# Paged attention of the sample rows starts at the output projection instead of beside the prompt's attention

## The chip, the cores and the metric

The kernel runs on one core of a Trainium2 chip. The metric is the device time of one execution in microseconds (us). Before the change three executions took 1454.08, 1442.74 and 1447.46 us; the median is 1447.46 us. A further execution was profiled.

## What is computed

One layer of a hybrid decoder, in float32, for two groups of rows at once.

- The **prompt**: 16 meta tokens and 1024 rows. RMSNorm, one input projection, differential attention with 4 heads of two softmax maps each (causal, with ALiBi), a gated depthwise convolution of width 31 with LayerNorm and swish, an output projection over both, a norm and the residual, then a SwiGLU feed-forward part (1024 to 2816 to 1024).
- The **samples**: 8 sequences with one new row each, which go through the same layer, but whose attention reads a paged cache: 32 pages of 128 keys per sequence. A page of keys and a page of values are 128 x 512 floats (256 KB) each, found through a page table. Cut to its core:

```
k_past = ck[page_table]; v_past = cv[page_table]
s = q . k * HEAD_DIM**-0.5 - slope * (q_pos - k_pos)
p = softmax(s);  a = p[map 0] - lam * p[map 1];  o = a @ v
```

All pages together are 512 transfers of 256 KB, 134 MB, of the 264 MB that the kernel moves.

## The kernel before

The prompt's work has four stages, written out in program order. First the projection stripes for the convolution and the convolution itself. Then the attention loop at the end of `tile_layer`: 32 blocks `n`, eight blocks of 128 query rows for each of four heads; between the blocks, `chunk_to` puts the remaining projection stripes of q, k and v, and these are all out by n = 22. Then the output projection, eight calls of `c_one` (the first at n = 31, inside the loop, the others behind it). Last the feed-forward part, `ffn`, which calls a helper `fill` 133 times between its groups of matmuls. Large products are made of three matmuls on the rounded value H and the rest L of each operand (`mm3`, L149 to L151).

In one attention block (`attn`) TensorE makes the scores (L507, L508), VectorE adds the bias and finds the extreme (L509), ScalarE takes the exponential (L515), VectorE joins the two maps (L526), TensorE transposes (L534), ScalarE copies (L538) and TensorE multiplies with the values (L548). GpSimd has the small powers of the norms (L125, L564), the L parts of some weights (L140) and of the keys (L300).

The samples' paged attention is a generator, `dec_units`, that other code advances by steps. A step is one pair of pages:

- **Keys** (128 steps): SyncE issues two page loads (`page_pair`, L665), GpSimd multiplies 128x1024 elements by the query (L679), VectorE sums them by head (L689).
- **Softmax**, once a sequence has its 16 key pairs: `dec_max` (L697 to L706, with a reduction over the partitions on GpSimd, L706), `dec_exp` (L711, L712), `dec_total` (L716).
- **Values** (128 steps): two page loads and, for two pairs side by side, eight matmul records with 8 columns of weights (L731).

The first 23 steps are keys only; from then on two value pairs alternate with two key pairs. When the generator is through, `fill` advances the sample rows' own layer (`sample_units`, 81 steps that read 512 KB of weights each).

`dec_step(rate)` adds `rate` to an account and takes as many whole steps. It is called in three places: in the attention loop from block `db` on, with `rate_b` of the head; in every `c_one`, with `rate_c`; in every `fill`, with `rate_d`. `fill` goes on with `rate_s` for the sample layer. The steps are put into the program at raised priority (400 instructions), and a planner that simulates a timeline orders the instructions of each engine. Each engine then works through its own list in that order and waits where an operand is late. The first load of each pair stands in the order behind the matmul last marked. Page buffers come from `kv`: four buffers until `kv_n[1]` is set behind the attention loop, then six more, which are the buffers `p` of the prompt's probabilities.

Of the kernel before, what the change touches and what calls it, by code (L numbers as in the profile page):

```python
# [46 lines left out]
def tile_layer(ctx: ExitStack, tc: tile.TileContext, I, O, cfg):  # L47
# [1339 lines left out]
    lag=7, rlag=1, elag=2,  # L1387
    xn_g=(), wi_first=1, wi_e=(13, 17), sq=0,
    behind=-400, w0=7, w1=7, wi_n=1, anchor=1, wi_v=(8, 9, 10, 11, 12), taps=11, conv=400, r2_g=1, hb=5,
    vgrp=2, fing=5, ml_g=0, fend=22, cst=0, db=3, cn=6, scn=12, wo0=27, wor=2, c0=7,  # L1390
    at=8, slabs=35, kv=4, p=6, dve_mul=0, rate_b=(1, 1.25, 1, 0.75), rate_c=1, rate_d=2.45, rate_s=2.2,
    ffn_l=lambda nc: nc.vector,
)
_INS = [
# [39 lines left out]
```

## Time and profile before

| | |
|---|---|
| median of three executions | 1447.46 us (1442.74 to 1454.08) |
| the profiled execution | 1442.33 us |
| its span, first to last instruction | 1440.6 us |
| TensorE (PE) busy | 1353.5 us, 94% |
| VectorE (DVE) busy | 876.8 us, 61% |
| ScalarE (ACT) busy | 552.2 us, 38% |
| GpSimd (POOL) busy | 560.5 us, 39% |
| moved by DMA | 264.35 MB, mean 183 GB/s |

The span is the profiled execution less 1.7 us around it. PE is busy nearly all the time, so the places to look at are those where it isn't. An engine's wait is named by what it waited for; a wait of an engine other than PE costs time only where PE in the end waits for it. Each engine works in order, so what stands behind a waiting instruction waits too.

### The profile page before, as it was taken

How to read it: one execution, taken by the hardware profiler on the slowest of the kernel's cores; microseconds unless marked ns; L12 is line 12 of the kernel's file. 1: busy time of each engine (PE TensorE's matmuls, PEld its weight loads, DVE VectorE, ACT ScalarE, POOL GpSimd, SP SyncE). 2: the span in 40 equal slices, each digit the busy share in tenths (PEclk: the TensorE clock that was granted, in tenths of full speed). 3: DMA queues.
4: the chain of work that ended last, by engine and by line, in shares of the span. 5: the costliest groups of instructions: out<-in, count | busy, mean ns of one | idle time of the engine just before them, and what ended most of it. 6: DMA issues, size and time to landing. Idle time of an engine off the chain costs nothing.

```text
span 1440.6 us, 21580 instructions
## 1 busy us (share of the span) xinstructions
PE 1353.5 (94%) x6960; PEld 1054.5 (73%) x6960; DVE 876.8 (61%) x1403; ACT 552.2 (38%) x1112; POOL 560.5 (39%) x351
## 2 busy tenths in 40 slices
PE   5999899979858999999999989999999999999997
PEld 5999799978746787777777667677676765666666
DVE  5689996945765467465748366565754265462158
ACT  7566978697855345212222121222122112211122
POOL 4598866444444123545445455454530000000023
PEclk9999999999979999999999999999999999999999
DMA  8221024226515538678777868687687656664454
GB/s 253 78 59 39 28 64 145 81 88 199 160 61 183 176 125 283 221 241 278 260 244 235 260 202 262 229 273 248 206 267 231 224 159 217 220 202 125 146 190 176
DMA packets 199678, 264.35 MB, mean 183 GB/s; under 512 B 16423, under 2 KB 99816, under 8 KB 199557
## 3 DMA queue, kind: packets, MB, share of 16 engines
q1 hardware_dynamic: 188912, 254.40, 54.1%
q10 hardware_dynamic: 10653, 8.57, 1.9%
q8 instruction: 55, 0.90, 0.3%
q14 instruction: 58, 0.48, 0.1%
HBM read 245.92 MB, written 17.48 MB: 183 GB/s over the span
## 4 chain that ended last, share of the span: by engine, by line
PE 61%; DMA 2%; issue 2%; DVE 2%; SPq 2%; POOL 1%; ACT 0%; POOLq 0%; DVEq 0%; ACTq 0%
PE pg L149 5%; PE pu L149 5%; PE pg L150 5%; PE pu L150 5%; PE pu L151 5%; PE pg L151 5%; PE dn L149 5%; PE dn L150 5%; PE dn L151 5%; PE pv L731 4%; PE mo L151 2%; PE mo L149 2%; PE mo L150 2%; DMA k<-in_cache_k 1%; POOL k L679 1%
## 5 line engine op out<-in xcount | busy, mean ns | idle before, releaser
L679 POOL TENSOR_TENSOR k<-k,qB 128x1024 f32<-128x1024 f32 x128 | 317.8, 2499 | 257.1 <-DMA k<-in_cache_k 212.0
L689 DVE TENSOR_REDUCE s<-k 128x16 f32<-128x1024 f32 x128 | 155.0, 1213 | 106.9 <-POOL k L679 106.8
L955 ACT CAST wH<-wr 128x1024 fp32r<-128x1024 f32 x66 | 69.1, 1049 | 249.1 <-DVE wL L957 142.6
L149 PE MATMUL dn<-wH,aH 128*128 128x512 f32 x352 | 141.2, 405 | 4.4 <-DVE y L998 2.7
L150 PE MATMUL dn<-wL,aH 128*128 128x512 f32 x352 | 140.9, 400 | 0.0
L149 PE MATMUL pu<-hH,wH 128*128 128x512 f32 x352 | 140.3, 399 | 0.5 <-DVE y L998 0.5
L151 PE MATMUL dn<-wH,aL 128*128 128x512 f32 x352 | 140.7, 400 | 0.0
L149 PE MATMUL pg<-hH,wH 128*128 128x512 f32 x352 | 140.4, 399 | 0.0
L151 PE MATMUL pu<-hH,wL 128*128 128x512 f32 x352 | 138.6, 395 | 1.5 <-DVE sm2n_t L123 1.5
L150 PE MATMUL pu<-hL,wH 128*128 128x512 f32 x352 | 139.5, 397 | 0.0
L150 PE MATMUL pg<-hL,wH 128*128 128x512 f32 x352 | 139.3, 396 | 0.0
L151 PE MATMUL pg<-hH,wL 128*128 128x512 f32 x352 | 139.2, 395 | 0.0
L957 DVE TENSOR_TENSOR wL<-wr,wH 128x1024 fp32r<-128x1024 f32 x66 | 97.1, 1471 | 38.0 <-ACT wH L955 21.6
L998 DVE TENSOR_TENSOR y<-dn,y 128x512 f32<-128x512 f32 x144 | 95.0, 684 | 35.4 <-PE dn L151 34.9
L414 POOL TENSOR_TENSOR cb<-cb 128x512 f32<-128x512 f32 x80 | 102.9, 1318 | 17.7 <-ACT cb L413 9.9
L423 DVE SCALAR_TENSOR_TENSOR acc<-u,cw,acc 128x512 f32<-128x512 f32 x144 | 98.8, 749 | 0.2
L1070 POOL TENSOR_TENSOR y<-y,wfpost 128x512 f32<-128x512 f32 x10 | 17.4, 1754 | 205.2 <-ACT ft L1068 205.1
L149 PEld LDWEIGHTS dn<-wH,aH 128*128 128x128 f32 x352 | 67.3, 192 | 31.2 <-DVE y L998 6.2
L981 ACT CAST aH<-sg 128x512 fp32r<-128x512 f32 x44 | 27.3, 621 | 163.2 <-DVE sg L974 163.1
L149 PEld LDWEIGHTS pu<-hH,wH 128*128 128x128 f32 x352 | 66.1, 188 | 27.8 <-issue 12.0
L149 PEld LDWEIGHTS pg<-hH,wH 128*128 128x128 f32 x352 | 66.1, 188 | 27.4 <-issue 11.6
L150 PEld LDWEIGHTS dn<-wL,aH 128*128 128x128 f32 x352 | 66.9, 190 | 25.1 <-issue 10.3
(581 smaller groups left out, 2947.3 us busy)
## 6 DMA issues: line engine op xcount, KB each, us to landing
k<-in_cache_k SPq DMA_DIRECT2D x256, 256.0 KB
v<-in_cache_v SPq DMA_DIRECT2D x256, 256.0 KB
wr<-in_w_gate SPq DMA_DIRECT2D x22, 512.0 KB
wr<-in_w_up SPq DMA_DIRECT2D x22, 512.0 KB
wr<-in_w_down SPq DMA_DIRECT2D x22, 512.0 KB
sd<-in_w_down SPq DMA_DIRECT2D x22, 512.0 KB
sw_gate<-in_w_gate SPq DMA_DIRECT2D x20, 512.0 KB
sw_up<-in_w_up SPq DMA_DIRECT2D x20, 512.0 KB
```

The lines of the kernel that those rows point to most:

```text
L149: T.matmul(out, lhsT=wH, rhs=xH, start=first, stop=False)
L150: T.matmul(out, lhsT=wH, rhs=xL, start=False, stop=False)
L151: mark(T.matmul(out, lhsT=wL, rhs=xH, start=False, stop=last))
L414: G.tensor_tensor(accp, accp, t, op=ALU.add)
L423: V.scalar_tensor_tensor(dst, src, cw[:, ct, k : k + 1], acc, op0=ALU.mult, op1=ALU.add)
L679: x = G.tensor_tensor(kt, kt, qB.unsqueeze(1).to_broadcast([P, 2, 512]), op=ALU.mult)
L689: x = V.tensor_reduce(s.rearrange("p a c -> p (a c)"), kt.rearrange("p a (c d) -> p (a c) d", d=HD), axis=AX.X, op=ALU.add)
L731: x = T.matmul(pv[32 * g : 32 * g + 8, :], lhsT=a[:, q + i, :], rhs=vt[:, i, :], start=q + i < 4, stop=q + i >= NPG - 4, tile_position=(0, ...
L955: S.copy(H[:, :1024], raw[:, :1024])
L957: V.tensor_tensor(L[:, :1024], raw[:, :1024], H[:, :1024].bitcast(F32), op=ALU.subtract)
L981: S.copy(aH, sg)
L998: V.tensor_tensor(y[b][:, ws], o, y[b][:, ws], op=ALU.add)
```

## The change

Four numbers change. With `db=32` the condition `n >= cfg["db"]` holds for no block of the loop, whose last n is 31, so `dec_step` is not called there any more and `rate_b` is without use. The call in `c_one` takes two steps instead of one, the one in `fill` 2.65 instead of 2.45, and the sample layer goes at 2.3 steps per `fill` instead of 2.2. No operation is added or removed.

```diff
-    vgrp=2, fing=5, ml_g=0, fend=22, cst=0, db=3, cn=6, scn=12, wo0=27, wor=2, c0=7,
-    at=8, slabs=35, kv=4, p=6, dve_mul=0, rate_b=(1, 1.25, 1, 0.75), rate_c=1, rate_d=2.45, rate_s=2.2,
+    vgrp=2, fing=5, ml_g=0, fend=22, cst=0, db=32, cn=6, scn=12, wo0=27, wor=2, c0=7,
+    at=8, slabs=35, kv=4, p=6, dve_mul=0, rate_b=(1, 1.25, 1, 0.75), rate_c=2, rate_d=2.65, rate_s=2.3,
```

The calls that these numbers steer, which stay as they are:

```python
        if n >= cfg["db"]:
            dec_step(cfg["rate_b"][h])
...
        dec_step(cfg["rate_c"])        # the end of c_one
...
        if dst["done"]:
            credit[0] += cfg["rate_s"]
...
        else:
            dec_step(cfg["rate_d"])    # in fill
```

## Rows read from the trace of the kernel before

**Rows 1.** Windows: length, busy us (count) of PE, PEld, DVE, ACT, POOL, clock, DMA, GB/s.
```profile
195.00:380.00 185.00, 171.27 (x1163) 164.96 (x1163) 122.89 (x296) 151.14 (x381) 90.14 (x60) 0.98 0.37 118
380.00:451.00 71.00, 42.61 (x250) 37.16 (x251) 49.31 (x120) 42.91 (x115) 32.95 (x17) 0.78 0.46 147
451.00:580.00 129.00, 129.00 (x616) 102.34 (x616) 75.35 (x128) 53.17 (x129) 29.86 (x25) 1.00 0.59 196
580.00:1140.00 560.00, 551.43 (x2546) 392.18 (x2545) 319.04 (x346) 112.34 (x150) 241.11 (x102) 0.99 0.74 244
1140.00:1430.00 290.00, 284.51 (x1320) 190.47 (x1320) 148.90 (x222) 57.54 (x97) 24.14 (x20) 0.99 0.54 179
```

**Rows 2.** PE in order of time, 380 to 460 us: start, length, operation [idle before].
```profile
402.07 1.16 PE L548 MATMUL o<-V,ats 128*128 128x128 f32 x8 [3.25 <-ACT ats L538]
...
415.57 0.75 PE L507 MATMUL S<-R,L 128*128 128x456 f32 x1 [5.23 <-DVE nm L509]
...
421.49 0.66 PE L507 MATMUL S<-R,L 128*128 128x352 f32 x1 [4.79 <-DVE nm L509]
...
444.52 0.47 PE L571 MATMUL oT<-ident,oh 128*128 128x128 f32 x1 [5.46 <-ACT oh L566]
```

**Rows 3.** DVE in order of time, the same stretch.
```profile
400.65 0.43 DVE L711 TENSOR_TENSOR s<-s,dg 128x264 f32<-128x264 f32 x1 [4.37 <-POOL dg L706]
...
413.27 1.22 DVE L689 TENSOR_REDUCE s<-k 128x16 f32<-128x1024 f32 x1 [5.75 <-POOL k L679]
...
415.94 4.78 DVE L526 SCALAR_TENSOR_TENSOR p<-p,cc,p 128x400 f32<-128x400 f32 x2
...
425.21 1.17 DVE L526 SCALAR_TENSOR_TENSOR p<-p,cc,p 128x400 f32<-128x400 f32 x2
...
437.73 5.43 DVE L526 SCALAR_TENSOR_TENSOR p<-p,cc,p 128x400 f32<-128x400 f32 x2
```

**Rows 4.** POOL in order of time, the same stretch.
```profile
410.91 4.64 POOL L679 TENSOR_TENSOR k<-k,qB 128x1024 f32<-128x1024 f32 x2
415.51 2.35 POOL L140 TENSOR_TENSOR wo3L<-wo3r,wo3H 128x1024 fp32r<-128x1024 f32 x1
...
437.48 2.36 POOL L679 TENSOR_TENSOR k<-k,qB 128x1024 f32<-128x1024 f32 x1
```

**Rows 5.** Groups by line (busy, mean ns | idle): 195 to 460 us twice, 460 to 580 us.
```profile
L679 POOL TENSOR_TENSOR k<-k,qB 128x1024 f32<-128x1024 f32 x26 | 61.7, 2383 | 19.3 <-DMA k<-in_cache_k 19.0
...
L689 DVE TENSOR_REDUCE s<-k 128x16 f32<-128x1024 f32 x24 | 29.1, 1214 | 8.8 <-POOL k L679 8.8
...
L679 POOL TENSOR_TENSOR k<-k,qB 128x1024 f32<-128x1024 f32 x8 | 20.2, 2535 | 22.9 <-DMA k<-in_cache_k 22.9
```

**Rows 6.** Waits of SP's queue, 380 to 460 us: total us, times, longest.
```profile
SPq L665 <- DVE s L689: 18.8, 2, 9.8
SPq L665 <- PE pv L731: 18.5, 1, 18.5
```

**Rows 7.** Groups by line, POOL, 580 to 1140 us.
```profile
L679 POOL TENSOR_TENSOR k<-k,qB 128x1024 f32<-128x1024 f32 x95 | 238.3, 2527 | 216.0 <-DMA k<-in_cache_k 171.3 <-issue 21.3 <-DVE s L689 12.8
```

**Rows 8.** Groups by line, DVE: 700 to 1050 us, then 1150 to 1390 us.
```profile
L957 DVE TENSOR_TENSOR wL<-wr,wH 128x1024 fp32r<-128x1024 f32 x27 | 46.3, 1716 | 11.1 <-PE pg L150 5.3 <-PE pu L150 3.9 <-ACT wH L955 1.2
...
L957 DVE TENSOR_TENSOR wL<-wr,wH 128x1024 fp32r<-128x1024 f32 x19 | 23.1, 1217 | 17.4 <-ACT wH L955 16.9 <-PE pu L151 0.5
```

**Rows 9.** Waits of DVE, 460 to 1141 us: total us, times, longest.
```profile
DVE s L689 <- POOL k L679: 98.0, 38, 6.7
```

**Rows 10.** The chain that ended last, in order of time: start, length, what.
```profile
831.80 4.39 DMA k<-in_cache_k
...
838.64 1.22 DVE s L689
...
862.82 0.97 PE pv L731 x8
...
1403.42 0.96 PE sd L1233 x4
```

## The prediction, made before the change was run

> **What bounds the kernel now.** I began with the busy shares and the 40 slices of the page, then asked for windows by stage. Five stages follow from them [rows 1]. PE is idle 13.7 us of 185 in the mixed part of the attention loop, and 28.4 us of 71 (71.00 less 42.61) in its last part, from 380 to 451 us, where no projection stripe is left to fill it and its clock was granted at 0.78 of full. In the output projection it is not idle at all. In the feed-forward part it is idle 8.6 us of 560 while pages are read, and 5.5 us of 290 afterwards. So the time is PE's work plus these holes, and a change that moves work without changing it can only win or lose in the holes. The reader should see that half of all idle time of PE from 195 us on lies in the 71 us before the output projection.
>
> The timelines of PE, DVE and POOL say what makes the holes there [rows 2 to 4]. Page work stands in the orders of DVE and POOL between the prompt's steps, and the prompt waits for it. The groups by line give its amount [rows 5], the waits of SP's queue and of DVE, with POOL's groups, its state in the other stages [rows 6, 7, 9].
>
> **How many steps move.** Before, the loop takes 5 + 10 + 8 + 6 = 29 steps (blocks 3 to 7 at 1, then eight blocks each at 1.25, 1 and 0.75) and the eight `c_one` take 8: 37, and 219 are left for the feed-forward part. After, the condition is true for no block, the eight `c_one` take 16, and 240 are left. At 2.45 and 2.65 per `fill` that is 89.4 and 90.6 fills of 133. The sample layer's 81 steps then take 36.8 and 35.2 fills, so it ends at fill 126.2 before and 125.8 after. The end of the program is thus left alone: the last sample matmul, now at 1403 us [rows 10], keeps its distance from it. I cost that at nothing; the cover is the six or seven fills behind it.
>
> **The attention loop, what is taken out.** 26 products of 2.38 us on POOL and 24 sums of 1.21 us on DVE, 62 and 29 us [rows 5], the first softmax, and one group of value matmuls, 0.97 us like each of these [rows 10]. Most of this ran beside other work. On the path are these holes of PE:
>
> - **First softmax.** DVE waits 4.37 us for the reduction on POOL [rows 3], ScalarE's copies stand behind that, and PE is idle 3.25 us [rows 2]. Gain 3.2.
> - **A sum in front of the bias.** DVE stands 5.75 us at a sum whose product is late on POOL [rows 3], the next L509 is behind it, and PE is idle 5.23 us [rows 2]. Gain 5.2.
> - **A stretched L526.** A pair of them takes 1.17 us at 425 us and 4.78 us at 416 us [rows 3], while POOL computes wo3L, which had stood behind two page products of 4.64 us [rows 4]. Without these, wo3L is over before DVE gets there. PE's hole is 4.79 us [rows 2]; bounds 0 and 4.8, I take 4.0, since 4.64 us of POOL's lateness are removed.
> - **The last L526 and the last norm.** 5.43 us beside a page product of 2.36 us and the last weight split [rows 3, 4]; PE's hole is 5.46 us [rows 2]. Bounds 0 and 5.5; the split stays, so I take the product, 2.4.
> - **The mixed part.** Bounds 0 and its 13.7 us of holes [rows 1]. PE is 93% busy there, so I take 2.0.
> - **Clock.** 42.6 us of PE work ran at 0.78 in the last part [rows 1]. All of it at full would give 42.6 x 0.22 = 9.4 us; nothing is the other end. Holes remain, and latency counts more than rate here, so I take 2.0.
>
> That is 18.8 us. **What is late next** is ScalarE, busy 42.9 of these 71 us [rows 1], and it has no page work worth naming. It must follow DVE more closely than now, so I give back 2: **16.8 us gained**.
>
> The stretch of L526 has a rule behind it. In the Trainium skill, "SBUF — State Buffer", section "SBUF: two separate sides", a VectorE operation with two SBUF inputs and a GpSimd operation exclude each other for a whole instruction. The trace agrees: 4.78 against 1.17 us [rows 3]. By the rule alone each of the 26 products could hold DVE for its full 2.38 us, 62 us in the loop; as DVE has slack there, the sum by the rows stands at 16.8. The same rule speaks against the change further on (third rival).
>
> **SP's queue.** The 58 or so page loads of the loop go. In the last part SP stood 37 us on page loads that waited for a free buffer [rows 6], with loads of the output weights and of the first block's inputs behind them. These come earlier. Bounds 0 and some us; the holes counted above contain what of it reached PE, so I add nothing.
>
> **The output projection.** 16 steps instead of 8, all keys: 16 products where 8 ran [rows 5], so 19 us more on POOL (busy 30 of 129) and 10 us more on DVE (75 of 129) [rows 1]. 16 more page loads stand on SP's queue among the next block's inputs; the longest wait of such a load for a sum was 9.8 us [rows 6], and an input is asked for one block, about 13 us, ahead. Bounds 0 and 9.8; I take 0, since PE has no hole there now and the cover is that one block. Without it a late input would stop PE at once. Four groups of value matmuls leave this stage, 3.9 us of PE, and return later: nothing.
>
> **The feed-forward part.** The value group that ran in a hole costs its 0.97 us now: +1.0. The pace per fill is 2.65 / 2.45 = 1.08 of before. DMA is busy 0.74 of the page part at 244 GB/s [rows 1]. Pages are 219 x 0.524 MB / 560 us = 205 of these, so after it is some 261 GB/s and 0.79. PE's holes of 8.6 us grow at least in proportion: +0.7. The upper bound is in the second rival. The waits show how near the edge this is: POOL stands 171 us for key pages [rows 7], and DVE 98 us at sums for POOL [rows 9], which reach PE seldom, as around 832 us, where a page, its sum and PE follow each other [rows 10].
>
> **Sum.** 16.8 - 1.0 - 0.7 = 15.1, some 1 us of SP's earlier loads not counted. The profiled execution took 1442.3 us, 5.1 under the median. 1447.5 - 15.1 gives 1432.4, and I round the uncounted part in: **1431 us**.
>
> **The rivals.**
>
> 1. **The freed time was not on the path.** The last part is held by the chain from scores over exponential to transposes, and ScalarE's 43 us with PE's round trips fill the 71 us anyway. For it: ScalarE stands in the chain of each block. Against it: three of PE's holes end at once with page work [rows 2, 3]. Gain 16.8 falls to some 3: 1447.5 - 3 + 1.7 = 1446.
> 2. **Late pages in the feed-forward part (slower).** A page buffer comes free only when its sum or its matmul is done, so 10 buffers bound the pace. If 219 steps in 560 us is already the most that this loop can do, 240 steps need 614 us, and the 90.6 fills would by themselves take 567: up to 47 us lost, so 1431 + 47 - 1 = 1477. It decides from a loss of 16 us on, that is, when the loop does less than 240 / 583 = 0.41 steps per us against 0.39 now. For it: POOL is behind the pages most of the time [rows 7]. Against it: DMA is not full, and between 451 and 580 us, with 0.59 of DMA busy, nothing holds PE. Half of the loss would give 1454.
> 3. **Half the gain is taken back.** 17 products more run beside the feed-forward part (112 against 95). A split of a weight takes 1.72 us beside the products and 1.22 us without [rows 8], so DVE loses up to 0.5 us for each, 8.5 us, and the sums take 21 us more. DVE is busy 319 of 560 us and waits 98 for products [rows 1, 9]; if the holes of PE double instead of growing by 8%, the time is 1431 + 8 = 1439. This is where the rule of the Trainium skill in "SBUF — State Buffer", "SBUF: two separate sides", would act again; the rows on the split agree with it.
>
> **Chances.** Forecast 0.52, with its own range of 1415 to 1438; first rival 0.13, second 0.17, third 0.18. A measurement of this kernel can't tell less than 1%, 14.5 us, from no change, so the bound for faster is 1433. The forecast is centred near it with more room below (the upper ends of the stretched L526, the clock and the mixed part, some 23 us together), so 0.37 of its 0.52 is faster and 0.15 is same; the first and third rivals are same but for 0.03 of the third; of the second 0.10 is slower (a loss of over 31 us) and 0.07 same. Faster 0.40, same 0.50, slower 0.10. The range is 1414 to 1457: below it lies 0.06, the loop's holes closing with the clock at full; above it 0.11, the second rival at more than half.
>
> **What would show it.** After: no L679 before about 420 us, the last part short by some 15 us with the clock above 0.9, no hole of PE before L548 and L507 that ends with page work; pairs of L526 near 1.2 us; in the output projection 16 products and PE still full; in the page part DMA near 0.79 and holes below 12 us. I am wrong if the last part is as long as now with ScalarE the releaser, if PE has holes in the output projection that end with a late input, or if PE waits for value pages and sums by tens of us.

## The result: 54 us slower, and the profile after

The changed kernel takes 1498.91 us (median of four executions, 1498.23 to 1500.48) where the kernel before takes 1445.14 (a fourth execution, of 1442.82 us, joined the three above). The ratio is 1.036, with a 95% interval of 1.031 to 1.041. The forecast was 1431 us with a range up to 1457: wrong in sign and outside its range.

The page of the kernel after, its first part and the PE line of its slices:

```profile
span 1496.5 us, 21608 instructions
## 1 busy us (share of the span) xinstructions
PE 1368.6 (91%) x6960; PEld 1062.5 (71%) x6960; DVE 880.2 (59%) x1403; ACT 555.2 (37%) x1116; POOL 555.4 (37%) x351
...
PE   5999899989689878969899997999999989999996
```

The PE line of the kernel before:

```profile
PE   5999899979858999999999989999999999999997
```

The work is the same (6960 matmul records both times), the holes are not. A slice is 37.4 us after and 36.0 us before. Of the 20 slices from 449 to 1197 us six have a PE digit under 9 after; before it was one of the 19 from 468 to 1153 us. They lie in the output projection and in the page part. To see where the time went I divided both traces at the same events: the first matmul of the output projection, the first of the down projection, the last group with value pages, the last of the down projection. Windows of the kernel after, divided there (columns as in [rows 1]):

```profile
195.00:431.50 236.50, 210.75 (x1427) 200.35 (x1426) 129.62 (x387) 196.94 (x498) 63.39 (x51) 0.95 0.24 75
431.50:617.40 185.90, 165.43 (x722) 129.29 (x721) 129.24 (x160) 57.71 (x135) 89.62 (x48) 0.94 0.58 191
617.40:1195.30 577.90, 541.33 (x2449) 378.23 (x2447) 311.75 (x345) 109.15 (x143) 240.32 (x106) 0.96 0.73 243
1195.30:1483.70 288.40, 279.42 (x1323) 189.15 (x1316) 147.14 (x216) 57.47 (x96) 21.11 (x20) 0.99 0.55 182
1483.70:1496.50 12.80, 0.43 (x2) 0.00 (x0) 7.40 (x15) 2.17 (x6) 1.10 (x2) 0.68 0.31 123
```

The kernel before, divided in the same way:

```profile
195.00:451.50 256.50, 214.38 (x1418) 202.61 (x1419) 172.49 (x414) 194.27 (x494) 123.08 (x76) 0.93 0.40 126
451.50:613.60 162.10, 162.10 (x770) 125.44 (x768) 92.63 (x146) 61.55 (x141) 49.98 (x34) 1.00 0.60 198
613.60:1138.10 524.50, 515.93 (x2385) 367.36 (x2381) 301.12 (x326) 102.55 (x134) 221.00 (x94) 0.99 0.75 247
1138.10:1432.10 294.00, 288.51 (x1342) 193.38 (x1335) 150.70 (x225) 59.46 (x101) 24.69 (x21) 0.99 0.54 180
1432.10:1440.60 8.50, 0.40 (x2) 0.00 (x0) 4.00 (x8) 0.72 (x2) 0.55 (x1) 0.82 0.32 123
```

The last part of the attention loop after, which took 71 us before [rows 1]:

```profile
380.00:431.50 51.50, 36.52 (x229) 31.77 (x230) 33.99 (x93) 38.39 (x104) 22.18 (x11) 0.83 0.37 124
```

The attention loop gives 20.0 us (256.5 to 236.5). Then 23.8 us are lost up to the first down projection (162.1 to 185.9) and 53.4 us in the page part (524.5 to 577.9). The two last stages give 5.6 (294.0 to 288.4) and lose 4.3 (8.5 to 12.8). That is -20.0 + 23.8 + 53.4 - 5.6 + 4.3 = 55.9 us, the difference of the spans. So the gain came as forecast, and two stages that I had costed at next to nothing took it back nearly four times over (77.2 us). Not all of this is holes: PE was busy 1368.6 us with the same records, 15.1 more than before, and idle 40.8 us more. The granted clock in the two stages that lost was 0.94 and 0.96 in the mean, before it was 1.00 and 0.99.

**The middle stage.** PE is idle 20.5 of 185.9 us and was never idle there. The three largest waits of PE, 460 to 600 us:

```profile
PE pg L151 <- DVE wL L957: 9.2, 2, 5.3
PE pu L151 <- DVE wL L957: 5.5, 1, 5.5
PE mo L151 <- DVE mL L900: 3.2, 2, 2.1
```

All three name VectorE. VectorE's groups in the same stage, 431.5 to 617.4 us, and then the same four operations before, 451.5 to 613.6 us:

```profile
L689 DVE TENSOR_REDUCE s<-k 128x16 f32<-128x1024 f32 x29 | 34.8, 1209 | 11.6 <-POOL k L679 11.6
L900 DVE TENSOR_TENSOR mL<-mx,mH 128x512 fp32r<-128x512 f32 (+1 forms) x14 | 18.7, 1369 | 0.4 <-ACT mH L899 0.4
L918 DVE SCALAR_TENSOR_TENSOR z<-xr,hr_r,wffn 128x1024 f32<-128x1024 f32 x8 | 16.6, 2075 | 3.8 <-POOL hr_r L125 3.8
L957 DVE TENSOR_TENSOR wL<-wr,wH 128x1024 fp32r<-128x1024 f32 x7 | 14.1, 2013 | 0.3 <-ACT wH L955 0.3
```

```profile
L689 DVE TENSOR_REDUCE s<-k 128x16 f32<-128x1024 f32 x16 | 19.3, 1212 | 8.8 <-POOL k L679 8.8
...
L918 DVE SCALAR_TENSOR_TENSOR z<-xr,hr_r,wffn 128x1024 f32<-128x1024 f32 x8 | 11.3, 1415 | 3.3 <-POOL hr_r L125 3.3
...
L900 DVE TENSOR_TENSOR mL<-mx,mH 128x512 fp32r<-128x512 f32 (+1 forms) x14 | 9.6, 727 | 0.2 <-ACT mH L899 0.2
L957 DVE TENSOR_TENSOR wL<-wr,wH 128x1024 fp32r<-128x1024 f32 x7 | 8.5, 1219 | 2.3 <-ACT wH L955 2.3
```

The sums are as long as ever (1.21 us), there are only more of them. The splits L900 and L957 have two inputs in SBUF, and their mean goes from 0.73 to 1.37 us and from 1.22 to 2.01 us, with the same count: they stand beside GpSimd's products. L918, a part of the norm, goes from 1.42 to 2.08 us. In order of time it looks like this on VectorE, and then on GpSimd:

```profile
502.96 4.05 DVE L900 TENSOR_TENSOR mL<-mx,mH 128x512 fp32r<-128x512 f32 x2
...
516.21 5.52 DVE L900 TENSOR_TENSOR mL<-mx,mH 128x512 fp32r<-128x512 f32 x2
...
530.40 3.38 DVE L918 SCALAR_TENSOR_TENSOR z<-xr,hr_r,wffn 128x1024 f32<-128x1024 f32 x1 [0.72 <-POOL hr_r L125]
533.70 3.35 DVE L957 TENSOR_TENSOR wL<-wr,wH 128x1024 fp32r<-128x1024 f32 x1
...
557.08 0.43 DVE L711 TENSOR_TENSOR s<-s,dg 128x264 f32<-128x264 f32 x1 [3.42 <-POOL dg L706]
...
568.36 1.22 DVE L689 TENSOR_REDUCE s<-k 128x16 f32<-128x1024 f32 x1 [8.11 <-POOL k L679]
569.50 2.22 DVE L957 TENSOR_TENSOR wL<-wr,wH 128x1024 fp32r<-128x1024 f32 x1
```

```profile
556.65 0.39 POOL L706 PARTITION_ALL_REDUCE dg<-dm  x1 [8.75 <-issue]
565.99 4.64 POOL L679 TENSOR_TENSOR k<-k,qB 128x1024 f32<-128x1024 f32 x2 [8.95 <-issue]
```

VectorE is late in two ways here. PE's holes for L900 (3.2 us in two) and the one of 5.3 us, which ends at 537 us, stand behind stretched operations: a pair of L900 takes 4.05 and 5.52 us (1.16 us in the kernel before, at 524 us), L918 and L957 take 3.4 us each. The other two holes for L957, 3.8 us (it ends at 559 us) and 5.5 us (at 572 us), stand behind waits of VectorE for GpSimd: 3.4 us for the reduction of a softmax (L706), 8.1 us for a product. GpSimd itself was idle 8.75 us ahead of that reduction and 8.95 us behind it, and the profile shows nothing that it waited for. By this, 8.5 of these 17.8 us follow a stretch and 9.3 us a pause of GpSimd around a reduction.

**The page part.** PE is idle 36.6 us against 8.6. The two largest waits of PE, 600 to 1200 us:

```profile
PE pv L731 <- DMA v<-in_cache_v: 14.7, 7, 9.9
PE dn L149 <- DVE y L998: 13.7, 5, 4.5
```

Pages are late, yet DMA is busy 0.73 of this stage, less than before (0.75). What comes ahead of the late pages is in the chain that ended last, here from 699 us on:

```profile
699.43 0.39 SPq L947
...
701.12 0.33 SPq L665
701.63 0.33 SPq L665
702.15 0.33 SPq L665
...
704.15 0.26 SPq L659
...
704.73 0.26 SPq L659
```

For some 20 us the chain is SyncE's own instructions, one behind the other with nothing waited for: a page load every 0.52 us, and a read of a page number (L659) every 0.57 us. A page costs SyncE 1.09 us and a step of two pages 2.18 us. The page of the profile doesn't list SyncE among its engines, for register and DMA-issuing instructions aren't counted as busy, and I had not added them up. At 2.45 steps and 6.61 us a fill (524.5 us over the 79.4 fills from the first down projection to the last pages) these two instructions fill 5.3 us of 6.6; at 2.65 steps 5.8 us, and weight loads and waits for free buffers come on top. The waits that the profile lists for SyncE's queue in the page part add up to 54 us of 524.5 before and 57 us of 577.9 after, so it was 0.9 full both times; and it issued 390 page loads before and 433 after, 0.74 and 0.75 a us. A pace 8% higher was asked for and did not come. The Trainium skill, "DMA: Bandwidth & Descriptors", section "Latency and other measured facts", puts the floor of such a read at about 600 ns; the spacing of 0.57 us lies just under it, and the 0.31 us that a read without the range check takes in e3 (0.83 less 0.52) well under it, so for the cost on the queue the measurement decides.

### The profile page after: what moved, and what is told of

Its sections match the earlier page's. It is cut to its first block, busy times and chain, and to the rows that moved or that the text cites. A ratio compares the mean times of both kernels' runs of the same rounds, so it can differ in the third digit from the quotient of the medians.

```text
span 1496.5 us, 21608 instructions
## 1 busy us (share of the span) xinstructions
PE 1368.6 (91%) x6960; PEld 1062.5 (71%) x6960; DVE 880.2 (59%) x1403; ACT 555.2 (37%) x1116; POOL 555.4 (37%) x351
## 4 chain that ended last, share of the span: by engine, by line
PE 40%; SPq 6%; DVE 5%; DMA 5%; issue 3%; POOL 2%; ACT 0%; POOLq 0%; DVEq 0%
PE pu L149 5%; PE pu L150 5%; PE pu L151 5%; PE pg L150 4%; PE pg L149 4%; PE pg L151 4%; SPq L665 3%; PE dn L149 3%; PE pv L731 3%; PE dn L150 3%; PE dn L151 3%; SPq L659 3%; DMA k<-in_cache_k 2%; POOL k L679 1%; DMA v<-in_cache_v 1%
## 5 line engine op out<-in xcount | busy, mean ns | idle before, releaser
L149 PE MATMUL pu<-hH,wH 128*128 128x512 f32 x352 | 145.3, 413 | 10.6 <-DVE y L998 5.8
L151 PE MATMUL pu<-hH,wL 128*128 128x512 f32 x352 | 142.0, 405 | 7.0 <-DVE wL L957 7.0
L150 PE MATMUL pu<-hL,wH 128*128 128x512 f32 x352 | 143.8, 409 | 0.0
L957 DVE TENSOR_TENSOR wL<-wr,wH 128x1024 fp32r<-128x1024 f32 x66 | 102.5, 1552 | 35.5 <-ACT wH L955 27.3
L998 DVE TENSOR_TENSOR y<-dn,y 128x512 f32<-128x512 f32 x144 | 95.9, 682 | 32.3 <-PE dn L151 31.6
L974 DVE TENSOR_TENSOR sg<-sg,pu 128x512 f32<-128x512 f32 x44 | 30.1, 683 | 107.5 <-PE pu L151 107.5
L1070 POOL TENSOR_TENSOR y<-y,wfpost 128x512 f32<-128x512 f32 x10 | 14.3, 1440 | 206.9 <-ACT ft L1068 206.8
L151 PEld LDWEIGHTS pg<-hH,wL 128*128 128x128 f32 x352 | 67.3, 191 | 28.5 <-DVE wL L957 10.0
```

The lines of the kernel that those rows point to most:

```text
L149: T.matmul(out, lhsT=wH, rhs=xH, start=first, stop=False)
L150: T.matmul(out, lhsT=wH, rhs=xL, start=False, stop=False)
L151: mark(T.matmul(out, lhsT=wL, rhs=xH, start=False, stop=last))
L957: V.tensor_tensor(L[:, :1024], raw[:, :1024], H[:, :1024].bitcast(F32), op=ALU.subtract)
L998: V.tensor_tensor(y[b][:, ws], o, y[b][:, ws], op=ALU.add)
```

## The experiments

My theory was that SyncE's queue limits the page part and VectorE, beside the products, the stage ahead of it. The rivals were the late start by itself (the pages lose a lead), and the ten page buffers or the DMA engines. In every experiment the planner orders all engines' work anew, so each is read by stages. The stages of all of them, from the same four events; a fill is counted from the first down projection to the end of the pages, and idle is that of PE in the page part:

| kernel | ratio to before (95%) | attention loop ends, us | to the first down projection | page part | fills | us a fill | idle |
|---|---|---|---|---|---|---|---|
| before | 1 | 451.5 | 162.1 | 524.5 | 79.4 | 6.61 | 8.6 |
| the change | 1.036 (1.031 to 1.041) | 431.5 | 185.9 | 577.9 | 80.6 | 7.17 | 36.6 |
| e1 start alone | 1.011 (1.006 to 1.016) | 429.8 | 156.7 | 630.8 | 91.2 | 6.92 | 29.9 |
| e2 rates alone | 1.021 (1.016 to 1.026) | 451.3 | 177.7 | 490.6 | 69.6 | 7.05 | 26.4 |
| e3 change, light reads | 1.018 (1.012 to 1.023) | 429.7 | 189.4 | 549.4 | 80.6 | 6.82 | 17.7 |
| e4 before, more reads | 1.067 (1.061 to 1.073) | 445.8 | 160.9 | 632.2 | 79.4 | 7.96 | 86.9 |
| e5 change, one a block | 1.015 (1.012 to 1.019) | 430.6 | 159.9 | 602.7 | 83.6 | 7.21 | 42.4 |
| e6 before, light reads | 0.997 (0.995 to 0.999) | 450.7 | 162.3 | 520.6 | 79.4 | 6.56 | 6.7 |
| e7 pause | 0.999 (0.997 to 1.001) | 438.8 | 160.8 | 559.9 | 83.5 | 6.71 | 15.8 |
| e8 late, light, old pace | 0.997 (0.995 to 0.999) | 431.1 | 159.7 | 597.1 | 91.2 | 6.55 | 7.6 |
| e9 change, no early products | 1.022 (1.019 to 1.024) | 430.5 | 169.0 | 571.3 | 80.6 | 7.09 | 31.0 |
| e10 late, light, 2.55 | 0.994 (0.992 to 0.996) | 430.1 | 160.2 | 586.2 | 87.3 | 6.71 | 15.8 |
| e11 pause, light | 0.998 (0.996 to 0.999) | 442.7 | 160.2 | 555.7 | 83.5 | 6.66 | 13.2 |
| e12 change, both undone | 0.985 (0.980 to 0.991) | 430.0 | 161.9 | 556.6 | 83.6 | 6.66 | 11.4 |

The page part alone doesn't compare kernels, since the number of fills in it differs; us a fill does.

**e1 and e2: the start alone, the rates alone.** From the kernel before, in e1 `db=3` became `db=32`; from the kernel after, in e2 `db=32` became `db=3`.

> Only db=32; the rates are those of before (1, 2.45, 2.2). 8 steps before the feed-forward part, 248 in it, so the page part takes 101 fills and some 11 of the sample layer's 81 steps are left for the end. Theory (SP's queue is the limit: one page costs it 0.51 us for the load and 0.57 us for reading its number, 2.17 us a step, and at 2.45 steps a fill it is 0.9 full): the output projection begins at about 431 us as with the whole change, no hole of PE over 5 us between 500 and 600 us, pages at 2.45 a fill keep their pace, about 6.4 us a fill, PE idle under 15 us in the page part; some 20 us are added at the end by the late sample steps: 1430 to 1455 us in all. Rival (it is the late start itself that costs, since the pages lose their lead): PE idle over 30 us in the page part and over 10 us between 500 and 600 us, over 1480 us in all.

> Only the rates (2, 2.65, 2.3); the pages start at the fourth block as before. 45 steps before the feed-forward part, 211 in it. Theory (SP's queue is full at this pace): the attention loop as long as before (output projection from about 451 us), a loss in the output projection and at the start of the feed-forward part of 10 to 25 us, and in the page part at least 2.3 us a step, PE idle over 20 us: 1465 to 1500 us. Rival (the late start costs): 1440 to 1455 us, PE idle under 12 us in the page part.

e1 took 1464.89 us, e2 1479.41. The rates lose by themselves, in both stages (+15.6 us and 26.4 us of idle PE), with the old start: that is the theory's case. In the middle stage of e2 the splits L957 are not stretched (1.22 us in the mean), and the stage is longer all the same. PE's longest hole of the middle stage, 7.6 us, stands behind VectorE, which waited for a small power of the norm that GpSimd computes (L125); GpSimd had been idle 9.3 us behind a softmax's reduction (the line of VectorE, then that of GpSimd):

```profile
559.38 1.28 DVE L918 SCALAR_TENSOR_TENSOR z<-xr,hr_r,wffn 128x1024 f32<-128x1024 f32 x1 [7.65 <-POOL hr_r L125]
```

```profile
558.76 0.59 POOL L125 TENSOR_TENSOR hr_r<-hr_t,mhalf 128x1 f32<-128x1 f32 x1 [9.30 <-issue]
```

But e1 misses: the start alone, at the old pace, has 29.9 us of idle PE in the page part, not under 15, and its 1465 us lies between the two expectations. Between 431 and 587 us it has no loss. So the late start does cost something in the page part, and this run can't say by what. e1 also shows its sample layer ending behind the rest: 31.2 us follow the last down projection, 8.5 before.

**e3 and e4: less and more on SyncE's queue.** e3, from the kernel after:

```
-  pts[0:1, n : n + 1], engines=[SP], min_val=0, max_val=n_pool - 1
+  pts[0:1, n : n + 1], engines=[SP], min_val=0, max_val=n_pool - 1, skip_runtime_bounds_check_because="..."
```

e4, from the kernel before, in front of the page load:

```
+            if i == 0:
+                more, _ = nc.values_load_multi_w_load_instructions(pts[0:1, n : n + 1], engines=[SP], ...)
+                lds = tuple(lds) + tuple(more)
```

> The whole change, but the page numbers are read without the range check, which takes two of the four instructions of each read from SP's queue (about 0.25 of 1.08 us a page). Nothing else of the data flow differs. Theory (SP's queue): it has 0.5 us a step to spare, the page part is paced by PE again, PE idle there under 15 us, 1445 to 1470 us in all. Rival (the ten page buffers, or the DMA engines, bound the pace): the page part as long as with the whole change, 1490 to 1500 us.

> The kernel before with one more read of a page number for every pair of pages, a value that nothing uses: 0.57 us more on SP's queue per step, 125 us over the 219 steps of the page part, and no more DMA, buffers or other engine's work. Theory (SP's queue is 0.9 full there): SP needs some 640 us for what took 560, so 1510 to 1545 us. Rival (buffers or DMA bound the pace): 1440 to 1455 us.

e4 took 1545.55 us, at the upper end of the theory's range and 97 us more than before, with the same DMA, buffers and work of the four compute engines. Its page part:

```profile
606.70:1238.90 632.20, 545.29 (x2402) 382.63 (x2404) 298.57 (x329) 104.94 (x136) 217.88 (x95) 0.93 0.64 206
```

107.7 us longer than before with DMA at 0.64: the queue that issues is the limit, not what carries the pages. The 197 added reads in this part, at 0.57 us each, are 112 us. e3 took 1474.20 us, 25 us less than the change, a little above the theory's 1470 and far from the rival's 1490; its idle PE, 17.7 us, is also a little above the 15 us forecast. Two page loads with their reads now follow within 0.83 us each (1.16 us is from the start of the first load to the end of the second):

```profile
703.21 1.16 SPq L666 DMA_DIRECT2D k<-in_cache_k  x2
```

and SyncE has time to stand and wait for buffers, as it had not: the waits listed for its queue add up to 150 us of 549.4, where they were 57 of 577.9 (its largest waits in the page part of the change, then of e3, where the added line moves L665 to L666 and L947 to L948):

```profile
SPq L665 <- DVE s L689: 26.1, 14, 4.7
SPq L945 <- DVE wL L957: 4.9, 2, 3.4
```

```profile
SPq L666 <- DVE s L690: 49.9, 18, 9.8
SPq L948 <- PE pu L151: 22.7, 7, 4.5
```

The page part falls from 577.9 to 549.4 us. The middle stage does not move (189.4 us), so its loss is not SyncE's.

**e5 and e9: what the middle stage pays for.** e5 is the change with `rate_c=1`; e9, from the kernel after:

```
-            x = G.tensor_tensor(kt, kt, qB...)
+            x = None
+            if n >= 23:
+                x = G.tensor_tensor(kt, kt, qB...)
```

> The whole change, but one step in each block of the output projection as before (rate_c=1). 8 steps ahead of the feed-forward part, 248 in it at 2.65: 93.6 fills. Theory (two costs: two steps a block hold up the output projection's inputs and the first weights, and SP's queue limits the pages to some 2.7 us a step later): from the first output projection to the first down projection 155 to 165 us instead of 186, PE idle there under 6 us; the page part still at about 2.7 us a step, so 1470 to 1485 us. Rival (what is lost between 500 and 600 us comes from the late start, not from this rate): over 175 us there, 1490 us or more.

> The whole change, but GpSimd's products of the first 23 key pairs are left out (the sums take the raw keys), so that loads, buffers and sums of the output projection's steps stay and only GpSimd's part goes; this changes the samples' scores of these pages. Theory (in the output projection VectorE's two-input operations are held up by the products beside them, some 21 us of stretch, and a sum waits for a late product): from the first output projection to the first down projection 160 to 172 us instead of 186; the rest as with the whole change, 1475 to 1487 us. Rival (the sums and the 16 more loads on SP's queue do it): 180 us or more there, 1492 to 1500 us.

e5 took 1470.88 us; the middle stage is back at 159.9 us with 3.5 us of idle PE, and the page part is as slow as with the change (7.21 us a fill). So one step a block instead of two undoes the whole loss of that stage, late start or not. e9 took 1477.03 us with 169.0 us in the middle stage: 17 of the 24 us go when only GpSimd's early products go, while the sums and loads stay. VectorE's splits in e9, 431 to 604 us, are short again:

```profile
L959 DVE TENSOR_TENSOR wL<-wr,wH 128x1024 fp32r<-128x1024 f32 x7 | 8.4, 1215 | 1.7 <-ACT wH L957 1.7
L902 DVE TENSOR_TENSOR mL<-mx,mH 128x512 fp32r<-128x512 f32 (+1 forms) x14 | 8.4, 619 | 0.7 <-ACT mH L901 0.7
```

1.22 and 0.62 us where the change has 2.01 and 1.37. So the products cause the hold-up, shown and not only inferred. But e9 takes away both ways of being late at once, the stretch and the sums that wait for a late product, and does not divide the loss between them. The stretch of L957 alone is not enough for a loss: in e5, where nothing is lost, it is longer than with the change.

```profile
L957 DVE TENSOR_TENSOR wL<-wr,wH 128x1024 fp32r<-128x1024 f32 x7 | 15.3, 2203 | 2.3 <-ACT wH L955 2.2
```

**e6, e7 and e11: was the kernel before limited too, and is a pause enough?** e6 is the kernel before with e3's lighter reads. e7 is the kernel before with `rate_b=(1, 1.25, 0.5, 0)`; e11 is e7 with the lighter reads.

> The kernel before with the page numbers read without the range check, 0.25 us less a page on SP's queue. Theory (SP's queue is 0.9 full before and becomes the limit only with the change): PE paces the page part already, so only its 8.6 us of holes can go: 1432 to 1446 us. Rival (SP's queue limits the kernel before as well): the page part 20 us shorter or more, under 1428 us.

> The kernel before with rate_b=(1, 1.25, 0.5, 0): pages start at the fourth block as before, but none is put beside the last head's eight blocks. 27 steps ahead of the feed-forward part, 229 in it at 2.45: 93.5 fills; the sample layer's 81 steps at 2.2 still fit. Theory (the 20 us that the change wins in the attention loop are those of its last part, where no stripe fills PE): the output projection begins at 430 to 438 us, and the early pages keep the later stages as they were: 1425 to 1440 us. Rival (the gain needs the whole loop free of pages): the output projection begins at 445 us or later, 1440 to 1455 us.

> The kernel of the early start with a pause beside the last head (rate_b 1, 1.25, 0.5, 0), with the lighter read of page numbers. Theory (the holes that the pause added to the page part, 15.8 us against 8.6, are SP's queue): page part idle under 9 us, 1428 to 1438 us. Rival (they come from the order of the work): as without the lighter read, 1439 to 1445 us.

e6 took 1442.81 us, as the theory had it: before the change SyncE's queue was nearly full and cost little. e7 took 1443.82 us and fits neither expectation well. It wins 12.7 us in the attention loop, between the two. The pause doesn't quite clear the last part: a product at 405.5 us and the first softmax's reduction at 395.7 us still stand there; that these are the 7 us that it lacks was not tried. It loses 7.2 us of idle PE in the page part again. e11 took 1443.08 us: its holes there (13.2 us, 12.8 of them PE waiting for VectorE's L998 in the down projection, now L999) did not go with the lighter reads, so these holes are not SyncE's. The theory missed there, and the time is in its rival's range.

**e8, e10 and e12: the pieces together.** e8 has the late start, the rates of before with `rate_s=2.65`, and the lighter reads; e10 the same with `rate_d=2.55, rate_s=2.35`; e12 is the change with `rate_c=1` and the lighter reads.

> The late start (db=32) with the rates of before (1, 2.45), the page numbers read without the range check, and 2.65 steps a fill for the sample layer so that it ends inside the feed-forward part. Theory (what the late start lost alone, 30 us of idle PE in the page part, is SP's queue, which can't make up for a late entry at 0.9 full): PE idle there under 15 us, 1405 to 1428 us. Rival (the late start costs by itself, by the lead that the pages lack): PE idle there 25 us or more, 1430 to 1450 us.

> A version that the runs so far point to: late start, one step a block, 2.55 and 2.35 a fill, page numbers read without the range check. The pages end at fill 97.3, and the sample layer needs 34.5 of the 35.7 fills that are left. Theory (with SP's queue relieved the pages can be a little faster than before without holes, and the sample layer needs no rush at its start): output projection from about 431 us, page part idle under 15 us, 1420 to 1436 us. Rival (any pace over 2.45 costs more than it gives back): 1438 to 1455 us.

> The whole change with both costs taken back at once: one step a block in the output projection, and page numbers read without the range check; 2.65 and 2.3 a fill stay. Theory (two separate costs, one in each stage): alone they gave 28 and 25 us, together they give their sum, 1440 to 1450 us, with 155 to 165 us from the first output projection to the first down projection and the page part idle under 25 us. Rival (one cost seen twice, a late entry that the later stage pays): together hardly more than one of them, 1460 us or more.

e8 took 1441.48 us. Its page part is what the theory said, and answers what e1 left open: the late start at the old pace has 7.6 us of idle PE once the reads are lighter, 29.9 us without. The total missed by 13 us and lies in the rival's range, for two reasons that no theory named: PE waits 8.7 us for the sample layer's first norm, and the sample layer ends last, so that 15.5 us follow the last down projection instead of 8.5. e10 took 1438.73 us and falls into its rival's range: 14.2 us of PE waiting for value pages, and the same late end. e12 took 1426.94 us, ratio 0.985 (0.980 to 0.991): 1.5% under the kernel before, and the only version here that is more than 1% under it. Its middle stage and its page part:

```profile
430.00:591.90 161.90, 155.80 (x705) 125.44 (x704) 116.09 (x154) 58.44 (x135) 73.43 (x43) 0.99 0.57 183
591.90:1148.50 556.60, 545.24 (x2535) 384.16 (x2533) 343.19 (x357) 113.23 (x148) 271.36 (x111) 0.99 0.80 265
```

The attention loop's 20 us are kept, the page part is at 6.66 us a fill against 6.61 before, and DMA carries 265 GB/s at 0.80, the load I had computed for the change. PE is idle 11.4 us in it, 10.9 of them for value pages, against 8.6 before. But I had expected 1440 to 1450 us. The two undone costs give 72 us together where they gave 28 and 25 alone. They are thus not independent: e5 alone made the page part no faster (7.21 us a fill), e3 alone made it 6.82, both make it 6.66. That a queue with no room lets any delay of the stage ahead stay, and a queue with room wipes it out, would explain it; it is argued from these three numbers and was not tried by itself.

## Why the prediction was wrong, step by step

1. **The attention loop: right.** Forecast 16.8 us, measured 20.0. The last part shrinks from 71 us to 51.5 (380 to 431.5 us), PE's holes there from 28.4 to 15.0 us; over the whole loop holes make up 16.4 of the 20.0 us, PE's busy time 3.6. Two signs named in the prediction did not come. The clock of the last part, forecast above 0.9, is 0.83. Pairs of L526, forecast near 1.2 us, still take 1.97 to 3.09 us where they stand beside one of GpSimd's weight splits (L140), which stayed; the two others take 1.03 and 1.30 us. So the sum fits better than its terms do.
2. **"I take 0, since PE has no hole there now": this step failed.** The output projection with the feed-forward part's beginning lost 23.8 us. I had bounded the term by one late input on SyncE's queue (9.8 us) and set no price on VectorE's lateness. The stretch and the wait for a reduction that I had read in [rows 3] and costed for the attention loop stood in the same trace, and I did not apply them to the stage into which the products were moved. Measured, L900, L957 and L918 took 20.0 us more than before (18.7 - 9.6, 14.1 - 8.5, 16.6 - 11.3), and PE's holes there, 20.5 us where there were none, follow in about equal parts these stretches and GpSimd's pauses around a reduction; e9 recovers 17 us by taking the early products away. The Trainium skill, "SBUF — State Buffer", section "SBUF: two separate sides", says that a VectorE operation with two SBUF inputs and a GpSimd operation that reads SBUF exclude each other for a whole instruction; the row of L900 agrees, 1.37 against 0.73 us.
3. **"They grow at least in proportion: +0.7": this step failed, and by most.** Holes went from 8.6 to 36.6 us, and the page part from 6.61 to 7.17 us a fill, over 80.6 fills some 45 us; what of it is not holes is more page work per fill and a longer matmul of the feed-forward part (0.404 us in the mean against 0.397) at the lower clock. I had sized DMA (0.79 of it, measured 0.73, as the pages came slower) and not the queue that issues it. The rows had it: I cited SP's waits [rows 6], counted "58 or so page loads" that go, and never multiplied a load by its length. What the runs showed in its place is a queue that did not go faster: 0.75 page loads a us where 0.74 had been. With the lighter reads it went to 0.79 (e3) and 0.82 (e12).
4. **The second rival had the price and the wrong cause.** It gave "up to 47 us lost" from the pace of before being the most, and the pace did stay nearly there, but the rival put that to the ten buffers. The buffers were the same in e3, e4 and e12, and the pace went where the queue's work went: 6.82, 7.96 and 6.66 us a fill. Its chance of 0.17 leaned on the argument that DMA was not full, which is no evidence about an issuing queue.
5. **The end: nearly right.** The sample layer, from its first matmul of the output projection to its last, went from 235.7 to 226.7 us, as the pace of 2.3 says; the end after the last down projection grew by 4.3 us, which was forecast as nothing.

Still open: how the loss of the middle stage divides between the stretch and GpSimd's pauses, what makes the down projection wait for VectorE in e7 and e11, and why the two costs together are worth 19 us more than their sum. To put part of the page loads on another engine's queue, which would relieve SyncE more than the lighter reads, was not tried. The Trainium skill says in "DMA: Bandwidth & Descriptors", section "Rules for kernel authors", that spreading DMAs over engines brings no bandwidth and only saves the issuing engine's time; no run here shows it, but that time is just what was short.

## What to carry to other kernels

Add up the issuing queue as if it were an engine: instructions per transfer, those that compute its address included, times their spacing, against the time that the stage has. When work leaves a stage, cost its hold-ups in the stage where it arrives with the same rows that showed them where it was. A resource that is 0.9 full at the old pace can't be scaled with the pace; the question is whether any room is left to catch up a delay.

## What the runs showed of the hardware

- One page load whose address comes from a table costs SyncE's queue 0.52 us, and reading its page number 0.57 us with the range check; without the check the two together take 0.83 us, and the changed kernel was 25 us shorter (e3).
- One read more for every two pages, with nothing else added, made the kernel 97 us longer (e4).
- VectorE's subtraction of two SBUF tiles (128x512 and 128x384, L900) took 1.37 us in the mean beside GpSimd's products and 0.62 us without them (the change and e9); the 128x1024 sum with one input stayed at 1.21 us in both.
- In the change GpSimd was idle 5.8 to 8.8 us ahead of each of the eight reductions over the partitions (0.39 us long) and 6.9 to 9.4 us behind each of the first seven, behind which its next work is a page product; for many of these pauses the profile shows nothing that it waited for.
